# The head of a two-layer diffusion block in single feature blocks: finer adaLN blocks, first projection one feature at a time, sums of squares added on the matrix engine

## The chip, the core and the metric

The kernel runs on one core of one Trainium2 chip. The metric is device time in microseconds (us) of one execution; a profiled execution also gives a span, from the first instruction to the last. Engines: PE (matrix products; PEld loads its weights), DVE (vector), ACT (activation), POOL, and SP, which here only issues DMAs. Each engine runs its own list of instructions in the order in which the program gave them out, and waits at an instruction until its inputs are there.

## The reference, cut to what matters

Two streams of 256 tokens, context and latent, of width 1024, go through two layers. What the change touches is the very beginning of layer 0:

```python
def rms_norm(x, w=None):
    y = x32 * lax.rsqrt(jnp.mean(x32 * x32, axis=-1, keepdims=True) + EPS)
...
    cond = jax.nn.silu(c)
    cond_c = jax.nn.silu(c_ctx)
    h, hc = x, ctx
    for l in range(DEPTH):
        mod = jnp.split((cond @ w_ada[l] + b_ada[l])[:, None, :], 6, axis=-1)
        mod_c = jnp.split(cond_c @ w_ada[l] + b_ada[l], 6, axis=-1)
        a = modulate(rms_norm(h, norm1_w[l]), mod[0], mod[1])
        ac = modulate(rms_norm(hc, norm1_w[l]), mod_c[0], mod_c[1])
        y, y_c = token_mixers(a, ac, ...)
```

So before the first projection can start, three things must exist: the inverse norm of each token, the first two (shift and scale) of the six adaLN vectors, and the modulated input `a`. The projection that comes first in the kernel is the one into the 416 (here 448) columns of latent attention.

## The kernel before, in words

All matrix products of weight kind are done in three passes, since operands are split into a high and a low part: high times high, high times low, low times high. `split` makes the parts of a weight (ACT copies the high part, DVE subtracts), `norm_block` makes those of the modulated input: DVE forms x, ACT adds the shift and writes the high part, DVE writes the low part. The model width of 1024 is eight feature blocks of 128, called f0 to f7 here; the 512 tokens are four tiles, of which tiles 2 and 3 are context (s = 1) and 0 and 1 latent (s = 0).

The head runs so. SP issues the loads, all on one queue: three small ones, then the four pieces of h, the parameters, and then by turns a block of the adaLN weights (four pieces of 512 KB, `load_ada0`) and a unit of the projection's weights (448 KB, `wdma`). At most eight loads are under way: each further one waits for the landing of the load eight places ahead of it. `square_sums` squares h and adds the pieces on DVE, and PE sums over the partitions with a column of ones; `rsqrt1` and `inv_diag` make the inverse norms on DVE; `broadcast` spreads them with PE into the PSUM tile `rb0`. `first_ada(b)` computes adaLN block b on PE, a pair of features in 512 columns, and `first_mod(b)` turns its row into columns (`cp`, small PE products), adds the bias on DVE and calls `norm_block` for both features and streams. `warm` issues products that nobody reads; they keep PE busy while it would wait.

The first projection is `agroup` over four units i = 0 to 3 of two features each. For each unit it goes over the tiles 2, 3, 0, 1 and for each over both features: 24 products of 448 columns, 96 in all. `first_hook` puts the rest of adaLN between them: after the second tile of unit i it calls `first_mod(i + 1)`, after the fourth `first_ada(i + 2)`. `load_rest`, called at the end of `first_ada(2)`, issues the loads of tables that are needed later, among them the mask `msk` (128 KB), which DVE converts at line 159 into the tile `mk`. After the projection come the wide products of the mixers (L229 to L231) and, between them, the preparation of latent attention (`mla_prepare`).

The order on each engine is set when the program is made, by a list scheduler that follows the text of the program and its own clock; `issue_after` pins an instruction behind another.

## Time and profile before

| | before |
|---|---|
| time, median of 3 runs (range) | 1559.16 us (1558.87 to 1565.18) |
| time of the profiled execution | 1562.33 us |
| its span | 1560.6 us |
| PE busy | 1539.3 us, 99% |
| DVE busy | 1182.4 us, 76% |
| ACT busy | 737.8 us, 47% |
| granted PE clock, mean | 0.998 |

A busy share near 100% of one engine says that the other engines matter only where PE waits for them. In the forty slices of the page PE stands at 8 in the first and the last and at 9 in all others, so what can be lost or won around the change lies in the first 60 us. The rows are copied further down.

### The profile page before, as it was taken

What the parts mean: (1) busy time and instruction counts of PE and PEld (TensorE: products, weight loads), DVE (VectorE), ACT (ScalarE), POOL (GpSimd) and SP (SyncE); (2) the same over time, 40 slices, a digit from 0 to 9 for tenths busy, and PEclk for the clock granted to TensorE, in tenths of its full rate; (3) what the DMA queues carried; (4) which work ended last, traced back from release to release, by engine and by line L of the source; (5) the groups of instructions that cost most, each with busy time, mean ns of one, the idle gap of its engine ahead of it and who ended that gap; (6) DMA issues with size and microseconds to landing.
All of it is one profiled execution on the core that took longest, in us unless ns stands there. A gap on an engine that the chain in (4) does not pass through costs nothing.

```text
span 1560.6 us, 25204 instructions
## 1 busy us (share of the span) xinstructions
PE 1539.3 (99%) x9410; PEld 1319.5 (85%) x9411; DVE 1182.4 (76%) x2931; ACT 737.8 (47%) x1504; POOL 13.8 (1%) x53
## 2 busy tenths in 40 slices
PE   8999999999999999999999999999999999999998
PEld 4887677877888889888888889987888799999998
DVE  5894457787899998668876776786688887896764
ACT  3665465353423333532332342556665364675553
POOL 1000000000000000000000000000000000000000
PEclk9999999999999999999999999999999999999999
DMA  9332112221344573236655563432234234555552
GB/s 368 125 108 68 55 46 70 76 77 64 112 154 141 204 259 125 91 121 202 191 190 200 189 194 118 137 106 68 83 99 127 71 133 151 188 164 192 182 185 88
DMA packets 63034, 215.56 MB, mean 138 GB/s; under 512 B 7104, under 2 KB 10560, under 8 KB 62912
## 3 DMA queue, kind: packets, MB, share of 16 engines
q1 hardware_dynamic: 62912, 213.95, 41.4%
q8 instruction: 74, 1.21, 0.3%
q14 instruction: 48, 0.39, 0.1%
HBM read 212.88 MB, written 1.05 MB: 137 GB/s over the span
## 4 chain that ended last, share of the span: by engine, by line
PE 69%; DVE 6%; issue 1%; ACT 1%; DMA 0%; DVEq 0%
PE pm L229 19%; PE pm L231 18%; PE pm L230 18%; PE pm L479 2%; PE pm L481 2%; PE pm L480 2%; PE pd L789 1%; DVE wl L226 1%; PE pd L645 1%; DVE junk L359 1%; PE pd L883 1%; PE pd L892 1%; PE pd L670 1%; DMA ar<-in_wadT_dram 0%; DVE u L742 0%
## 5 line engine op out<-in xcount | busy, mean ns | idle before, releaser
L229 PE MATMUL pm<-u,wh 128*128 128x256 f32 (+1 forms) x1868 | 645.0, 346 | 1.1 <-ACT wh L225 1.1
L231 PE MATMUL pm<-u,wl 128*128 128x256 f32 (+1 forms) x1868 | 632.0, 339 | 1.8 <-DVE wl L226 1.8
L230 PE MATMUL pm<-u,wh 128*128 128x256 f32 (+1 forms) x1868 | 631.8, 339 | 0.0
L225 ACT ACTIVATE wh<-raw 128x512 fp32r<-128x512 f32 (+1 forms) x526 | 310.4, 619 | 447.1 <-PE pm L230 306.1
L226 DVE TENSOR_TENSOR wl<-raw,wh 128x512 fp32r<-128x512 f32 (+1 forms) x526 | 344.8, 679 | 108.0 <-ACT wh L225 103.3
L229 PEld LDWEIGHTS pm<-u,wh 128*128 128x128 f32 x1868 | 354.8, 190 | 41.5 <-issue 3.2
L231 PEld LDWEIGHTS pm<-u,wl 128*128 128x128 f32 x1868 | 354.5, 190 | 40.7 <-DVE wl L226 2.4
L230 PEld LDWEIGHTS pm<-u,wh 128*128 128x128 f32 x1868 | 355.2, 190 | 38.2 <-issue 1.4
L359 DVE SCALAR_TENSOR_TENSOR junk<-ar,crow 128x512 bf16<-128x512 f32 x256 | 166.4, 690 | 4.4 <-DMA ar<-in_wadT_dram 4.4
L479 PE MATMUL pm<-wh,u 128*128 128x512 f32 (+3 forms) x304 | 117.2, 386 | 0.9 <-DVE s L1071 0.9
L481 PE MATMUL pm<-wh,u 128*128 128x512 f32 (+3 forms) x304 | 111.6, 370 | 0.0
L480 PE MATMUL pm<-wl,u 128*128 128x512 f32 (+3 forms) x304 | 111.1, 366 | 0.0
L1181 DVE SCALAR_TENSOR_TENSOR u<-pm,modT,u 128x256 f32<-128x256 f32 x96 | 44.4, 482 | 59.8 <-PE pm L231 59.6
L479 PEld LDWEIGHTS pm<-wh,u 128*128 128x128 f32 x304 | 57.3, 189 | 14.8 <-issue 3.8
L480 PEld LDWEIGHTS pm<-wl,u 128*128 128x128 f32 x304 | 57.4, 189 | 11.4 <-issue 4.7
L481 PEld LDWEIGHTS pm<-wh,u 128*128 128x128 f32 x304 | 57.3, 189 | 9.7 <-issue 1.4
L229 PE MATMUL pm<-u,w 128*128 128x256 f32 (+1 forms) x220 | 62.7, 285 | 0.0
L231 PE MATMUL pm<-u,w 128*128 128x256 f32 (+1 forms) x220 | 62.5, 284 | 0.0
L230 PE MATMUL pm<-u,w 128*128 128x256 f32 (+1 forms) x220 | 62.3, 283 | 0.0
L225 ACT ACTIVATE w<-raw 128x512 fp32r<-128x512 f32 (+1 forms) x68 | 39.1, 611 | 26.7 <-PE pm L230 15.6
L647 DVE TENSOR_REDUCE st<-pd 128x1 f32<-128x512 f32 (+1 forms) x48 | 28.6, 598 | 27.2 <-PE pd L645 26.9
L1270 DVE TENSOR_TENSOR s<-s,pm 128x512 f32<-128x512 f32 (+1 forms) x42 | 23.5, 561 | 33.6 <-PE pm L231 25.1
(263 smaller groups left out, 1906.7 us busy)
## 6 DMA issues: line engine op xcount, KB each, us to landing
raw<-in_wu_dram SPq DMA_DIRECT2D x256, 512.0 KB, 3.5
ar<-in_wadT_dram SPq DMA_DIRECT2D x80, 512.0 KB, 4.2
raw<-in_wu_dram SPq DMA_DIRECT2D x40, 448.0 KB, 3.3
u<-in_wad_dram SPq DMA_DIRECT2D x16, 512.0 KB, 10.1
u<-in_hin_dram SPq DMA_DIRECT2D x8, 512.0 KB, 6.3
raw<-in_wqb_dram SPq DMA_DIRECT2D x4, 384.0 KB, 3.4
raw<-in_wkvb_dram SPq DMA_DIRECT2D x2, 512.0 KB, 5.5
crow<-in_crow_dram SPq DMA_DIRECT2D x2, 512.0 KB, 4.8
```

What stands on the lines that cost most here:

```text
L225: ACT.activation(out=hi, in_=src, func=AF.Copy)
L226: paced[0] = DVE.tensor_tensor(out=lo, in0=src, in1=hi.bitcast(F32), op=ALU.subtract)
L229: PE.matmul(o, lh, rh, start=start, stop=False, **kw)
L230: PE.matmul(o, lh, rl, start=False, stop=False, **kw)
L231: PE.matmul(o, ll, rh, start=False, stop=stop, **kw)
L359: DVE.scalar_tensor_tensor(out=junk[:, sl], in0=raw[:, sl], scalar=1.0, in1=crows[s][:, sl], op0=ALU.mult, op1=ALU.mult, accum_out=part[:, ...
L479: PE.matmul(o, ah, wh, start=first, stop=False)
L480: PE.matmul(o, ah, wl, start=False, stop=False)
L481: PE.matmul(o, al, wh, start=False, stop=last)
L647: DVE.tensor_reduce(out=mx, in_=ps[:, :W], axis=AX.X, op=ALU.max, negate=True)
L1181: DVE.scalar_tensor_tensor(out=hx, in0=ps[:, 256 * s:256 * s + 256], scalar=G[:, f, s:s + 1], in1=hx, op0=ALU.mult, op1=ALU.add)
L1270: DVE.tensor_tensor(out=cv[:, :nq], in0=cv[:, :nq], in1=pu[:, :nq], op=ALU.mult)
```

## The change

The numbers of squares, adaLN weights, products and converted weights stay the same; how they are cut and in which order they stand changes.

- The loads of h go first, the three small loads behind them. The adaLN weights of the first four features are laid out feature by feature; all sixteen pieces and three of the four weight units are issued ahead of the other loads. The parameters of layer 1 move forward, the mask moves behind the weights of latent attention.
- `square_sums`: DVE adds no pieces; PE adds them in PSUM, with 16 one-column products for each stream instead of 4. The inverse norms of the two streams are computed one after the other instead of in one interleaved chain of four.
- adaLN comes in six blocks instead of four: f0, f1, f2, f3 (256 columns each), f4 with f5, f6 with f7 (512 columns each).
- The first two units of the projection go feature by feature over all tiles, the others tile by tile as before. `ADA_AT` and `MOD_AT` say after which (unit, feature of it, tile count) a block and its `first_mod` come.
- The conversion of the projection's weights and `mla_prepare` are pinned behind the norm steps. There are 28 of the products that nobody reads instead of 37.

```diff
     h = {s: load_h(s) for s in (1, 0)}
+    nc.sync.dma_start(out=craw, in_=cond)
+    nc.sync.dma_start(out=cs[:, K_ID:K_ID + 128], in_=cst[:, K_ID:K_ID + 128])
+    nc.sync.dma_start(out=cs[:, K_SEL:K_SEL + 2], in_=cst[:, K_SEL:K_SEL + 2])
...
-        nc.sync.dma_start(out=pr[1], in_=par[1])
...
-            split(hi[:, c0:c1], lo[:, c0:c1], raw[:, c0:c1])
+            held = last_mod if 3 < i < 8 else ()
+            with tc.issue_after(held[0]) if held else nullcontext(), tc.issue_after(held[1]) if held else nullcontext():
+                split(hi[:, c0:c1], lo[:, c0:c1], raw[:, c0:c1])
...
-        wload(i + 1)
+        if i > 2:
+            wload(i + 1)
...
+            if hook and i < 2:
+                for kk in range(2):
+                    for n, t in enumerate(tiles):
+                        product(t, (kk,))
+                        hook(i, kk, n + 1)
+                continue
...
     def square_sums(s):
-        acc = None
...
+        for n in range(4):
+            sq = T3([128, 2, 256])
+            x = h[s][n // 2][:, 2 * (n % 2):2 * (n % 2) + 2]
+            if n % 2 == 0 or (s == 0 and n == 3):
+                ACT.activation(out=sq, in_=x, func=AF.Square)
+            else:
+                paced[0] = DVE.tensor_tensor(out=sq, in0=x, in1=x, op=ALU.mult)
+            for j in range(2):
+                for i in range(2):
+                    with ordered():
+                        ins = PE.matmul(ps[:, j:j + 1], sq[:, i, j * 128:(j + 1) * 128], ones[:, 0:1], start=(n + i + j == 0),
+                                        stop=(n == 3 and i == 1), skip_group_check=True)
+                    seg.append(ins)
...
-    ada0 = [load_ada0(0)]
+    ada0 = [[], [], [], []]
+    load_ada0(0, 0, 2)
     wdma(0)
-    ada0.append(load_ada0(1))
+    load_ada0(0, 2, 4)
+    nc.sync.dma_start(out=pr[1], in_=par[1])
+    load_ada0(1, 0, 2)
     wdma(1)
+    load_ada0(1, 2, 4)
+    load_ada0(2)
+    wdma(2)
+    load_ada0(3)
+
+    BLOCKS = ((0, 1), (1, 1), (2, 1), (3, 1), (4, 2), (6, 2))
...
-        if 0 < b < 3:
-            wdma(b)
-            ada0.append(load_ada0(b + 1))
...
+        if b == 3:
+            wdma(3)
+            load_rest()
...
-        row = ACT.activation(out=first_row[b], in_=ps, func=AF.Copy)
-        if b == 2:
-            wdma(3)
-            load_rest()
+        row = ACT.activation(out=first_row[b][:, :w], in_=ps[:, :w], func=AF.Copy)
...
-    warm(8)
+    warm(6)
     ps0 = square_sums(0)
...
-    row0 = first_ada(0, lambda: warm(4))
...
+    first_ada(0, lambda: warm(2))
+    broadcast(1, dg1)
+    broadcast(0, dg0)
...
-    warm(5)
-    first_ada(1)
...
+    def first_hook(i, kk, n):
+        at = (i, kk, n)
+        if at in ADA_AT:
+            first_ada(ADA_AT.index(at) + 1)
+        if at in MOD_AT:
+            b = MOD_AT.index(at) + 1
+            with tc.issue_after(paced[0].ins):
+                act, dve = first_mod(b)
+            last_mod[:] = act.ins, dve.ins
+            if b in (1, 3, 4):
+                with tc.issue_after(act.ins), tc.issue_after(dve.ins):
+                    wload({1: 1, 3: 2, 4: 3}[b])
+
+    ADA_AT = ((0, 0, 1), (0, 0, 4), (0, 1, 4), (1, 1, 3), (2, 1, 3))
+    MOD_AT = ((0, 0, 2), (0, 1, 2), (1, 0, 2), (1, 1, 4), (2, 1, 4))
...
-        S = mla_prepare(l)
+        with tc.issue_after(last_mod[0]) if full else nullcontext(), tc.issue_after(last_mod[1]) if full else nullcontext():
+            S = mla_prepare(l)
```

How the order on the engines changes is shown at three places. A row is a line of the program, the operation, out<-in by the program's names, and the shape.

The first place is the queue of SP from the last adaLN pieces (`in_wad`) on. Behind them come the fourth weight unit (128x896), tables (`in_cst`), the mask (`in_msk`), the weights of latent attention (`in_wkvb`, `in_wqb`) and the fifth unit (128x1024). Before:

```order
L951 DMA u_414<-in_wad_dram 128x1024
L247 DMA raw_427<-in_wu_dram 128x896
L156 DMA cs<-in_cst_dram 128x128
L158 DMA s_430<-in_msk_dram 128x256
L160 DMA cs<-in_cst_dram 128x1536
L161 DMA pr_96<-in_par_dram 128x262
L247 DMA raw_564<-in_wu_dram 128x1024
L495 DMA raw_596<-in_wkvb_dram 128x1024
L495 DMA raw_604<-in_wqb_dram 128x768
```

And now:

```order
L958 DMA u_158<-in_wad_dram 128x1024
L156 DMA cs<-in_cst_dram 128x128
L247 DMA raw_428<-in_wu_dram 128x896
L160 DMA cs<-in_cst_dram 128x1536
L508 DMA raw_637<-in_wkvb_dram 128x1024
L508 DMA raw_645<-in_wqb_dram 128x768
L247 DMA raw_605<-in_wu_dram 128x1024
L158 DMA s_431<-in_msk_dram 128x256
```

The mask, the 30th load of the program before, is the 35th now, behind the tables, the weights of latent attention and the fifth unit; the same 35 loads stand first in both.

The second place is DVE around the conversion of the mask (`mk`). Before, it stands between the norm steps of f4 and f5 (x is L413, the low part L415, the weight's low part L226):

```order
L413 SCALAR_TENSOR_TENSOR s_478<-u_92,st_468,pd_127 128x256
L415 SCALAR_TENSOR_TENSOR u_125<-s_470,modT_115,u_121 128x256
L415 SCALAR_TENSOR_TENSOR u_125<-s_474,modT_115,u_121 128x256
L413 SCALAR_TENSOR_TENSOR s_482<-u_92,st_468,pd_127 128x256
L159 CAST mk<-s_430 128x256
L415 SCALAR_TENSOR_TENSOR u_125<-s_478,modT_115,u_121 128x256
```

Now it stands between x (L416) and the low part (L418, `u_409`) of f3:

```order
L1012 SCALAR_TENSOR_TENSOR st_464<-modT_115,pr_95 128x2
L416 SCALAR_TENSOR_TENSOR s_467<-u_84,st_464,pd_119 128x256
L416 SCALAR_TENSOR_TENSOR s_471<-u_88,st_464,pd_119 128x256
L159 CAST mk<-s_431 128x256
L418 SCALAR_TENSOR_TENSOR u_409<-s_467,modT_115,u_408 128x256
L418 SCALAR_TENSOR_TENSOR u_409<-s_471,modT_115,u_408 128x256
L225 TENSOR_TENSOR wl_476<-raw_150,wh_475 128x448 x2
```

It moved one pair of features forward, ahead of the low part of f3 and of the third unit's weight.

The third place is PE where the projection goes from one unit to the next. Before, at unit 2 (`wh_443`), the `cp` products of f6 and f7 (L992) have twelve products of the same unit behind them:

```order
L481 MATMUL pm_348<-wh_443,u_125 128x448
L992 MATMUL pd_527<-cs,s_507 128x2 x4
L479 MATMUL pm_349<-wh_443,u_121 128x448
L480 MATMUL pm_349<-wl_444,u_121 128x448
L481 MATMUL pm_349<-wh_443,u_125 128x448
L479 MATMUL pm_349<-wh_443,u_121 128x448
```

Now, from the third feature's partner f3 (`wh_376` with `u_408`, `u_409`) to unit 2 (`wh_475`):

```order
L485 MATMUL pm_342<-wh_376,u_409 128x448
L988 MATMUL pd_496<-u_142,cnd 32x512 x2
L988 MATMUL pd_496<-u_144,cnd 32x512 x2
L988 MATMUL pd_496<-u_146,cnd 32x512 x2
L988 MATMUL pd_496<-u_148,cnd 32x512 x2
L483 MATMUL pm_343<-wh_376,u_408 128x448
L484 MATMUL pm_343<-wl_377,u_408 128x448
L485 MATMUL pm_343<-wh_376,u_409 128x448
L1003 MATMUL pd_510<-cs,s_505 128x2 x4
L483 MATMUL pm_340<-wh_475,u_515 128x448
```

The `cp` products of f4 and f5 (L1003) are the last of unit 1 now, and the next product reads f4 itself (`u_515`); the same holds for f6 and f7 between units 2 and 3. Behind the first 345 of PE's rows, 281 of DVE's, 107 of ACT's and 36 of SP's, the orders of both kernels are the same.

## Rows read from the trace of the kernel before

**Rows 1.** Part 1 of the page: engine, busy us, share, instructions.
```profile
PE 1539.3 (99%) x9410; PEld 1319.5 (85%) x9411; DVE 1182.4 (76%) x2931; ACT 737.8 (47%) x1504; POOL 13.8 (1%) x53
```

**Rows 2.** A stretch: busy of PE, PEld, DVE, ACT, POOL, granted clock, DMA share, GB/s.
```profile
25.00:30.00 5.00, 5.00 (x30) 3.58 (x30) 2.19 (x7) 2.04 (x4) 0.00 (x0) 1.00 1.03 409
```

**Rows 3.** PE's timeline: start, length, line, operation, tiles, count, idle before.
```profile
1.53 6.17 PE L913 MATMUL pd<-resetf,wones 128*128 128x512 bf16 x20 [1.53 <-POOL resetf L179]
9.40 1.02 PE L933 MATMUL pd<-ones,y 128*128 128x1 f32 x8 [1.70 <-DVE y L928]
10.28 1.89 PE L913 MATMUL pd<-resetf,wones 128*128 128x512 bf16 x8
...
21.45 0.47 PE L479 MATMUL pm<-wh,u 128*128 128x448 f32 x1
...
39.13 1.93 PE L972 MATMUL pd<-u,cnd 128*32 128x512 f32 x16
...
43.56 0.95 PE L992 MATMUL pd<-cs,s 128*128 128x2 f32 x8
44.37 0.45 PE L479 MATMUL pm<-wh,u 128*128 128x448 f32 x1
...
51.68 0.37 PE L481 MATMUL pm<-wh,u 128*128 128x448 f32 x1
51.89 0.40 PE L229 MATMUL pm<-u,wh 128*128 128x512 f32 x1
```

**Rows 4.** SP's timeline: the first load, h, and the 35th load.
```profile
0.74 0.40 SPq L138 DMA_DIRECT2D st<-in_cond_dram  x1
...
2.12 1.85 SPq L145 DMA_DIRECT2D u<-in_hin_dram  x4
...
35.53 0.33 SPq L495 DMA_DIRECT2D raw<-in_wqb_dram  x1
```

**Rows 5.** Line 495, issue at 35.5 alone: from issue to landing.
```profile
DMA to landing us min/median/max: 7.5/7.5/7.5
```

**Rows 6.** Line 145, the first piece of h alone: from issue to landing.
```profile
DMA to landing us min/median/max: 3.6/3.6/3.6
```

**Rows 7.** DVE's and ACT's timelines: first norm steps, and the mask's conversion.
```profile
19.46 0.23 DVE L998 TENSOR_TENSOR modT<-pd,pr 128x4 f32<-128x4 f32 x2 [0.26 <-PE pd L992]
...
41.00 0.28 DVE L159 CAST mk<-s 128x256 uint8<-128x256 f32 x1
41.20 0.48 DVE L415 SCALAR_TENSOR_TENSOR u<-s,modT,u 128x256 fp32r<-128x256 f32 x1
...
20.45 1.71 ACT L414 ACTIVATE u<-s,modT 128x256 fp32r<-128x256 f32 x4 [1.97 <-DVE s L413]
```

**Rows 8.** Two stretches of PE alone: busy, granted clock, DMA share, GB/s.
```profile
1213.00:1217.00 4.00, 2.07 (x16) 0.97 0.00 0
1217.00:1220.00 3.00, 3.00 (x17) 0.50 0.00 0
```

**Rows 9.** Products of 256 columns there, from PE's timeline.
```profile
1212.65 0.28 PE L229 MATMUL pm<-u,wh 128*128 128x256 f32 x1
1213.26 0.28 PE L231 MATMUL pm<-u,wl 128*128 128x256 f32 x1
...
1217.62 0.41 PE L231 MATMUL pm<-u,wl 128*128 128x256 f32 x1
1218.68 0.41 PE L230 MATMUL pm<-u,wh 128*128 128x256 f32 x1
```

**Rows 10.** DVE's timeline at a later norm: two inverse norms, first and last steps.
```profile
605.60 0.21 DVE L205 TENSOR_SCALAR st<-pd 128x1 f32<-128x1 f32 x2
...
607.53 0.48 DVE L405 TENSOR_SCALAR s<-cs,st 128x128 f32<-128x128 f32 x2
```

**Rows 11.** Issue to landing: fourth weight unit (issued 26.8), table behind it (64 KB, 28.0).
```profile
DMA to landing us min/median/max: 9.9/9.9/9.9
...
DMA to landing us min/median/max: 8.9/8.9/8.9
```

More of the change, by code (lines that the diff above doesn't have):

```diff
@@ L413, in norm_block @@
         DVE.scalar_tensor_tensor(out=x, in0=hx, scalar=A_, in1=rb, op0=ALU.mult, op1=ALU.mult)
-        ACT.activation(out=hi, in_=x, func=AF.Identity, bias=B_)
-        return DVE.scalar_tensor_tensor(out=lo, in0=x, scalar=B_, in1=hi.bitcast(F32), op0=ALU.add, op1=ALU.subtract)
+        act = ACT.activation(out=hi, in_=x, func=AF.Identity, bias=B_)
+        return act, DVE.scalar_tensor_tensor(out=lo, in0=x, scalar=B_, in1=hi.bitcast(F32), op0=ALU.add, op1=ALU.subtract)
     def norm_half(s, acc, A, B, aT, raw=None):
@@ L480, in agroup @@
                     PE.matmul(o, ah, wl, start=False, stop=False)
-                    PE.matmul(o, al, wh, start=False, stop=last)
-                tick(6 * (c1 - c0) / 2.4)
+                    last_mm[0] = PE.matmul(o, al, wh, start=False, stop=last)
+                tick(3 * len(kks) * (c1 - c0) / 2.4)
+            if hook and i < 2:
[4 more added lines that the diff above has]
+                continue
+            for n, t in enumerate(tiles):
+                product(t, (0, 1))
                 if hook:
-                    hook(i, n + 1)
+                    hook(i, 1, n + 1)
         return pss
@@ L994, in first_mod @@
                 seg.append(ins)
-        f0 = 2 * b
-        md = modT[0][:, 0:2, f0:f0 + 2]
-        for m in range(2):
-            DVE.tensor_tensor(out=md[:, m], in0=cp[:, 2 * m:2 * m + 2], in1=bias_cols(0, m, f0, f0 + 2, 2), op=ALU.add)
-        A = ST(4).rearrange("p (f s) -> p f s", s=2)
+        if f0 % 2 == 0:
+            for x in aT:
+                x.append(U([128, 2, 512], F32R))
+        md = modT[0][:, 0:2, f0:f0 + nf]
+        DVE.tensor_tensor(out=md[:, 1], in0=cp[:, nf:], in1=bias_cols(0, 1, f0, f0 + nf, 2), op=ALU.add)
@@ new lines, in first_mod @@
+        if b == 0:
+            with tc.issue_after(ins.ins):
+                first_split(0)
+        with tc.issue_after(paced[0].ins) if b == 0 else nullcontext():
+            for j in range(nf):
+                for s in (1, 0):
+                    f = f0 + j
+                    hi, lo = aTs(aT, f, 256 * s, 256 * s + 256)
+                    ins = norm_block(h[s][f // 4][:, f % 4], A[:, j, s:s + 1], md[:, 0, j, s:s + 1], rb0[:, 256 * s:256 * s + 256], hi, lo)
+        if b == 0:
+            with tc.issue_after(ins[1].ins):
+                first_split(1)
@@ L1009, with first_split @@
+        return ins
+    def first_split(half):
+        raw, n = raws[0]
+        if not half:
+            loaded[0] = tuple(wp.tile([128, 1024], F32R, tag=x, bufs=3, name=nm(x)) for x in ("wh", "wl"))
+        hi, lo = loaded[0]
+        sl = slice(half * n // 2, (half + 1) * n // 2)
+        split(hi[:, sl], lo[:, sl], raw[:, sl])
+        if half:
+            raws.pop(0)
     warm(20)
     ps1 = square_sums(1)
-    warm(8)
+    warm(6)
     ps0 = square_sums(0)
+    dg1 = inv_diag(ps1)
     with tc.issue_after(paced[0].ins):
-        dg = inv_diag([ps[:, j:j + 1] for ps in (ps1, ps0) for j in range(2)])
```

84 lines of the change are left out of this document (27 added, 57 removed).

## The prediction

> **What bounds the kernel now.** I read the busy shares first: PE works in 99% of the span, the next engine in 76% [rows 1], so only what moves PE moves the time. Then I read PE's own order of time in the first 60 us, because the two programs differ nowhere else. After a start with gaps (the products that nobody reads run until about 7.5 us, and PE then waits for DVE's sums, 1.7 us at 9.40) the first product of the projection comes at 21.45, and from there PE has hardly a gap: the last of the 96 stands at 51.68, the first wide product of the mixers at 51.89 [rows 3]. Between them lie 96 products at 0.21 us each (51.68 to 51.89) = 19.9 us, and some 9 us of adaLN and `cp` work. Third, the loads: in a stretch of that time the DMA engines are full and move 409 GB/s [rows 2]. So the head has two walls, PE's work and a full load queue. In the kernel before, PE's work is the later one. All that follows is the question when the first wide product comes: 51.9 now. Behind it the order on each engine is soon the same, and PE goes on without waits, so I take a shift there to reach the end in full.
>
> **Part 1, h first and sums on PE.** The first piece of h is issued at 0.74 instead of 2.12 [rows 4] and so lands 1.4 us earlier. PE does not profit. The first 20 idle products end where they did, at 7.5 us, and behind them PE now has 16 one-column products per stream instead of 4. Eight records (4 products) took from 9.40 to 10.28, 0.88 us [rows 3], so a stream costs 3.5 us instead of 0.9. 7.5 + 3.5 + six idle products at 0.22 (the first to last of 8 took 1.89 us including the last one's end) 1.3 + 3.5 = 16 us for the second stream's sums. Its inverse norms are a chain of two, 2.4 us by the chain of two elsewhere in the trace, 605.60 to 608.01 [rows 10]. 18.5; broadcast and two `cp` products 0.9; then DVE's bias, half a weight conversion of 0.6 us that now stands in between, x, and ACT's high part: 2.2 us. First product: 21.7, so 0.3 us later than now. It takes 5 us more of PE to save nothing, but nothing was lost either.
>
> **Part 2, finer blocks on PE.** adaLN of 512 columns costs 1.93 us [rows 3]. Half of it in 256 columns costs between 0.97 and 1.93; I take 1.05, as the columns should set it. Before, a half block was done ahead of 21.45; now three half blocks and two whole ones follow the first product: 7.0 us against 6.8. `cp` (0.8 us for four columns, 43.56 to 44.37) is 3.0 against 2.4 us. The products are the same. So PE's work grows by some 0.8 us.
>
> **Part 3, norm steps without cover.** From a `cp` to the first product that reads the feature, DVE and ACT need: 0.2 us from the start of the next thing on PE to DVE's bias (the last record of `cp` ends at 43.56 + 0.95 = 44.51, 0.14 after the product behind it starts, and a step to DVE), then 19.46 to the end of ACT's first high part, 20.45 + 0.5 = 20.95, thus 1.5 us, and a step to PE [rows 7]. Before, twelve products (2.5 us) stood behind each `cp`; for f1 and f2 other products and adaLN still do. For f4 and f6 nothing does: `cp` is the last thing of its unit and the next product reads f4 (or f6) itself. That is 1.75 us of waiting, twice, and about 0.3 us for f3. Without part 4 the first wide product would come at 51.9 + 0.3 + 0.8 + 3.8 = 56.8 minus small change, some 4.6 us later than now. This would be 1564 us.
>
> **Part 4, the mask.** This is the term that decides. DVE's conversion of the mask is a wait of a new size: it stands ahead of the low part of f3, on an engine that runs its list in order, and the mask is now the 35th load instead of the 30th. When does it land? The same 35 loads were the first in the kernel before; the last of them was issued at 35.5 and landed 7.5 us later, at 43.0 [rows 4, 5]. The stream now starts 1.4 us earlier and has three small loads (73 KB, 0.2 us at that rate) in it: 41.8. A lower bound: the sizes by their shapes add up to 15.1 MB; at 409 GB/s [rows 2] this is 36.9 us; the first piece, 512 KB or 1.3 us, landed 3.6 us after its issue [rows 6], so the flow begins at 3.1 and ends at 40.0. I take 41.8, since a stream with all its hiccups was measured.
>
> PE gets to f3 at about 34.5: 21.7, 36 products 7.4 us, three half blocks 3.2, three `cp` 1.3, steps between them 0.9. It can do the products with f3's high part, not those with its low part, and all of PE's list stands behind them; so do, on DVE, the low part itself, the third unit's weight and all later norms. PE waits some 7 us, four times the wait at 9.40. How early PE and DVE came to this place no longer matters: parts 1 and 2 before f3 are swallowed.
>
> From the landing (M = 41.8) to the first wide product: conversion 0.28 and low part 0.48 [rows 7] with their steps, 0.8; nine products of f3, 1.9; adaLN of f4 and f5 2.0; row still on ACT, 0.1; `cp` 0.8; norm steps 1.75; eighteen products 3.9 with small waits for low parts; adaLN of f6 and f7 2.0; six products 1.25; `cp` 0.8; norm steps 1.75; 24 products 5.2. Sum 22.3, so 64.1.
>
> The clock comes on top. [...] A stretch like 1217 to 1220 at 0.50, and a little more, loses 3.3 x (1 - 0.12 / 0.21) = 1.4 us; I add 1.5, between 0 and 4.5 if the two later waits cost a dip each.
>
> Sum: 41.8 + 22.3 + 1.5 = 65.6, against 51.9: 13.7 us later. The profiled execution took 1562.33 us, 1.7 us over its span, and 3.2 us over the median of the runs; by it the time would be 1576, by the median of 1559.16 it is **1573 us**. I see no slack later: PE's remaining waits are short and come from other chains. I forecast slower.
>
> [...] The table issued at 28.0 landed at 36.9, right behind a weight unit issued at 26.8 that landed at 36.7 [rows 11]: 64 KB waited for 448 KB ahead of it, so loads land in the order of their issue here. [...]
>
> **The rivals.**
> - *Mask out of order.* If the mask overtook the queue, it would land as soon as it can be issued (it waits for the load eight places ahead; from that one's landing to its own there are 3.4 MB, 8.3 us, so that is 33.5) plus a landing time like the 3.6 us of a load with an empty queue: 37, with PE waiting 2 us at f3 instead of 7, and no dip. 1573 - 4.8 - 1.5 = 1567. Chance 0.05; the landings in order speak against it.
> - *The conversion holds nothing up* (the mask comes before PE needs f3's low part, that is before 35). Then parts 1 to 3 stand alone: 1564. It needs a stream 7 us faster than the full rate. Chance 0.08.
> - *The head is faster, as it is cut to be.* One feature at a time lets PE start as soon as f0 is ready. If the one-column sums ran as fast as the pieces of h come in, they would end near 10.5 us, with h landed 1.4 us earlier, and the projection would start some 3 us earlier; minus the waits at f4 and f6 that is -1 to 0 us: 1558. It decides at the sums: over 0.17 us per one-column product it is gone, and 0.22 was measured; the mask must be in time too. Chance 0.05. More than 7.8 us can't be won by it: the first product would have to come before 13.7, and the sums alone, at the speed measured, are done at 16.
> - *More dips.* Both waits at f4 and f6 also drop the clock: 1576. Chance 0.12.
>
> **How the numbers follow.** Forecast 1573 with 0.70. Its own bounds are 41.8 or 40.0 for the mask and 0 or 1.5 for the clock: 1570 to 1574. With the dips the upper end is 1577; below, 1565 takes in the overtaking mask and leaves the cases near 1564 and 1558 out. Half a per cent, 7.8 us, is about what a measurement of this kernel can tell from no change. Slower by more than that, over 1567: 0.70 + 0.12 + half of the overtaking mask = 0.84. Within: 0.13. Faster by more: 0.03, for what I have not seen.
>
> **What would show it.** Right: DVE's conversion of the mask starts at 40 to 42 with a long wait that a load ended; PE has one gap of 5 to 8 us between products of f3, then a granted clock near 0.5; gaps of 1.5 to 2 us behind the `cp` of f4 and f6; first wide product at 62 to 67. Wrong: the conversion at about 34 without a wait, or the mask landed before loads issued ahead of it. The sums of squares should end near 16 and the first product come near 21.7; whether they do says who is right on parts 1 and 2, and hardly changes the time.

## The result, and the profile of the changed kernel

| | kernel before | changed kernel |
|---|---|---|
| median of 6 executions each, us | 1561.25 (1558.87 to 1565.18) | 1578.39 (1574.62 to 1581.0) |
| profiled execution, us | 1562.33 | 1575.72 |
| its span, us | 1560.6 | 1573.9 |
| first product of the projection at, us | 21.45 | 27.17 |
| first wide product of the mixers at, us | 51.89 | 65.50 |

The ratio is 1.0109, with a 95% interval of 1.0096 to 1.0121: the changed kernel is 17 us slower. The forecast was 1573 us in a range of 1565 to 1577. The direction and most of the size were right, the time lies 1.4 us above the range. The profiled execution is the second fastest of the six.

The first things to read are again PE's busy time and its granted clock in 40 slices (parts 1 and 2 of the page of the changed kernel).

```profile
PE 1549.0 (98%) x9482; PEld 1331.0 (85%) x9482; DVE 1181.2 (75%) x2933; ACT 735.1 (47%) x1504; POOL 12.5 (1%) x53
...
PEclk7999999999999999999999999999999999999999
```

PE is busy for 9.7 us more than in [rows 1] with 72 instructions more, and the first slice, the head, ran at a granted clock of 0.7. PE's timeline of the head (start, length, line, operation, tiles, count, idle before) shows where:

```profile
1.52 6.04 PE L926 MATMUL pd<-resetf,wones 128*128 128x512 bf16 x20 [1.52 <-POOL resetf L178]
7.39 3.63 PE L940 MATMUL pd<-ones,y 128*128 128x1 f32 x32
10.88 2.11 PE L926 MATMUL pd<-resetf,wones 128*128 128x512 bf16 x6
12.79 6.82 PE L940 MATMUL pd<-ones,y 128*128 128x1 f32 x32
...
27.17 0.74 PE L483 MATMUL pm<-wh,u 128*128 128x448 f32 x1 [1.92 <-ACT u L417]
...
42.05 0.47 PE L483 MATMUL pm<-wh,u 128*128 128x448 f32 x1 [0.16 <-ACT u L417]
...
60.28 0.47 PE L483 MATMUL pm<-wh,u 128*128 128x448 f32 x1 [1.51 <-ACT u L417]
65.50 0.40 PE L228 MATMUL pm<-u,wh 128*128 128x512 f32 x1
```

The same 32 records (16 one-column sums) took 3.63 us for the first stream and 6.82 us for the second. The stretches say why (columns as in [rows 2]); first the changed kernel, then the kernel before:

```profile
4.00:11.00 7.00, 7.00 (x48) 5.16 (x47) 2.08 (x3) 3.24 (x7) 1.36 (x8) 1.00 1.04 401
11.00:17.00 6.00, 6.00 (x28) 5.01 (x25) 2.53 (x23) 0.00 (x0) 0.46 (x2) 0.54 1.03 407
17.00:24.00 7.00, 7.00 (x35) 4.26 (x35) 2.42 (x21) 1.33 (x4) 0.00 (x0) 0.50 1.02 406
24.00:32.00 8.00, 6.08 (x30) 3.93 (x29) 3.25 (x11) 1.37 (x4) 0.00 (x0) 0.50 1.03 408
32.00:41.00 9.00, 9.00 (x70) 6.88 (x71) 5.81 (x20) 3.40 (x8) 2.32 (x8) 1.00 0.88 344
41.00:52.00 11.00, 9.33 (x48) 6.34 (x47) 6.57 (x18) 4.59 (x10) 0.00 (x0) 0.87 0.16 50
```

```profile
11.00:17.00 6.00, 5.03 (x33) 1.91 (x32) 5.07 (x42) 0.07 (x2) 2.26 (x7) 1.00 1.03 416
17.00:24.00 7.00, 6.49 (x36) 3.56 (x36) 5.64 (x18) 3.19 (x7) 0.00 (x0) 1.00 1.03 406
```

From about 11.5 to 32 us PE ran at a granted clock of 0.50, with 1.00 before and behind (the lower and the higher level below). It had not idled: from 4 to 11 it was busy in 7.00 of 7.00 us. In the kernel before, PE was busy less in the same stretches (5.03 of 6.00 and 6.49 of 7.00 us) and kept 1.00.

The timelines of VectorE (DVE) and SyncE (SP) show the mask, on which the forecast stood (on SyncE the issue of the fifth weight unit and of the mask behind it, then the conversion and the low part of f3 on VectorE):

```profile
35.97 0.33 SPq L247 DMA_DIRECT2D raw<-in_wu_dram  x1
36.34 0.43 SPq L158 DMA_DIRECT2D s<-in_msk_dram  x1
```

```profile
41.77 0.29 DVE L159 CAST mk<-s 128x256 uint8<-128x256 f32 x1
42.03 0.89 DVE L418 SCALAR_TENSOR_TENSOR u<-s,modT,u 128x256 fp32r<-128x256 f32 x2
```

The load took 5.3 us from issue to landing, so it landed at 41.67, and the conversion began 0.1 us later, without a wait. That this is so near the forecast's 41.8 is luck. SyncE held the unit ahead of the mask back until 35.97, by the profile 3.9 us of it for VectorE's low parts of an earlier weight unit (L225), which ended at 35.94: the slow head delayed the load itself. In the executions below with an earlier first product (e1, e8, the second one of the changed kernel) the mask was issued at 34.0 and landed at 42.3 to 42.4. In this execution PE came to f3 at 42.05, when the mask had just landed: the slow start had used up all the time for which the mask would have held PE. The first wide product came at 65.50, where 65.6 was forecast, but on another path than the forecast's. From there on nothing changed: the span ends 1573.9 - 65.5 = 1508.4 us later, before 1560.6 - 51.9 = 1508.7.

So one execution agrees with the forecast in its number and not in its cause. The runs had to tell which of the two, the clock or the mask, sets the time, and whether one hides the other. The expectations below use these names. **Theory A** (e1 to e4): the one-column sums take the clock down and this sets the head, while the mask, landing at the same 42 us, only just holds nothing up; either alone taken away gives nothing. Against it stand **the theory of the prediction**, the mask alone, for which early work doesn't matter, and **theory B**, the clock alone. **Theory C** (from the second execution of the changed kernel on): the clock costs up to 10 us in the head, at a time that varies, and the mask is a second wall at 42 us; whichever is later counts. **Rival N:** the clock falls from the number of small products, or from the finer blocks.

### The profile page after: what moved, and what is told of

Its sections match the earlier page's. It is cut to its first block, busy times and chain, and to the rows that moved or that the text cites. A ratio compares the mean times of both kernels' runs of the same rounds, so it can differ in the third digit from the quotient of the medians.

```text
span 1573.9 us, 25350 instructions
## 1 busy us (share of the span) xinstructions
PE 1549.0 (98%) x9482; PEld 1331.0 (85%) x9482; DVE 1181.2 (75%) x2933; ACT 735.1 (47%) x1504; POOL 12.5 (1%) x53
## 3 DMA queue, kind: packets, MB, share of 16 engines
HBM read 212.88 MB, written 1.05 MB: 136 GB/s over the span
## 4 chain that ended last, share of the span: by engine, by line
PE 69%; DVE 5%; issue 1%; ACT 1%; DMA 1%; DVEq 0%
PE pm L228 19%; PE pm L230 19%; PE pm L229 19%; PE pm L483 2%; PE pm L485 2%; PE pm L484 2%; PE pd L802 1%; PE pd L658 1%; DVE junk L362 1%; PE pd L905 1%; PE pd L896 1%; DVE wl L225 1%; PE pd L683 1%; DMA ar<-in_wadT_dram 1%; DVE u L755 0%
## 5 line engine op out<-in xcount | busy, mean ns | idle before, releaser
L225 DVE TENSOR_TENSOR wl<-raw,wh 128x512 fp32r<-128x512 f32 (+1 forms) x526 | 344.0, 676 | 107.1 <-ACT wh L224 102.7
L228 PEld LDWEIGHTS pm<-u,wh 128*128 128x128 f32 x1868 | 354.4, 190 | 41.4 <-issue 3.2
L483 PEld LDWEIGHTS pm<-wh,u 128*128 128x128 f32 x304 | 58.0, 191 | 20.6 <-ACT u L417 6.7
L224 ACT ACTIVATE w<-raw 128x512 fp32r<-128x512 f32 (+1 forms) x68 | 39.0, 610 | 26.8 <-PE pm L229 15.7
```

The source lines that it names most:

```text
L224: ACT.activation(out=hi, in_=src, func=AF.Copy)
L225: paced[0] = DVE.tensor_tensor(out=lo, in0=src, in1=hi.bitcast(F32), op=ALU.subtract)
L228: PE.matmul(o, lh, rh, start=start, stop=False, **kw)
L483: PE.matmul(o, ah, wh, start=first, stop=False)
```

## The experiments

All times are against the kernel before on the same chip (its medians there were 1560.7 to 1562.5 us). "First" and "wide" are the starts of the first product and of the first wide product in the profiled execution.

| run | what is changed | first | wide | median us | ratio, 95% interval |
|---|---|---|---|---|---|
| changed kernel | | 27.17 | 65.50 | 1578.39 | 1.0109 [1.0096, 1.0121] |
| e4_before_pe_sums | before + sums on PE | 29.54 | 59.85 | 1568.15 | 1.0044 [1.0026, 1.0061] |
| e1_dve_adds | VectorE adds | 20.73 | 68.54 | 1577.41 | 1.0105 [1.0074, 1.0136] |
| e2_mask_late | late mask | 23.68 | 61.40 | 1574.75 | 1.0083 [1.0060, 1.0106] |
| e3_adds_and_mask | both | 18.70 | 57.29 | 1567.26 | 1.0038 [1.0027, 1.0050] |
| e5_fill | unread products among the sums | 28.70 | 69.12 | 1577.19 | 1.0101 [1.0087, 1.0114] |
| e8_wide_sums | sums of 128 columns | 21.85 | 65.96 | 1577.47 | 1.0099 [1.0083, 1.0116] |
| e10_wide_and_late | e8 + late mask | 21.89 | 59.56 | 1570.41 | 1.0069 [1.0052, 1.0085] |
| e6_fillers_head | e3 + unread products | 19.43 | 55.74 | 1565.53 | 1.0031 [1.0019, 1.0042] |
| e7_cover | e6 + f4, f6 earlier | 19.43 | 50.45 | 1560.80 | 0.9995 [0.9986, 1.0003] |
| e9_cp_first | e7 + `cp` ahead of a broadcast | 20.07 | 51.13 | 1559.34 | 0.9985 [0.9976, 0.9994] |

### The sums alone, in the kernel before

The kernel before with one part of the change, `square_sums` of the changed kernel, 16 products per stream for 4; with it, two of the eight squares go from ScalarE to VectorE (the loads of h stay where they were):

```diff
-    paced[0] = DVE.tensor_tensor(out=acc, in0=acc, in1=sq, op=ALU.add)
...
-    ins = PE.matmul(ps[:, j:j + 1], acc[:, i, j * 128:(j + 1) * 128], ones[:, 0:1], start=(i == 0), stop=(i == 1))
+    ins = PE.matmul(ps[:, j:j + 1], sq[:, i, j * 128:(j + 1) * 128], ones[:, 0:1], start=(n + i + j == 0),
+                    stop=(n == 3 and i == 1), skip_group_check=True)
```

> The kernel before with one part of the change alone: the pieces of the squares added by PE, 16 one-column products per stream. Theory A: the clock falls in the head here too, behind the first or in the second stream's sums; those take near 7 us instead of 3.5, the first product of the projection comes 6 to 9 us later than 21.45, the time grows by 7 to 10 us. If the products' number is what counts and not the clock: clock high throughout, 5.3 us more of PE of which 2.4 fall into waits, time plus 3 us.

Measured: 0.44% slower, 7 us, as theory A had it. The sums' rows and the first product in PE's timeline, then two stretches:

```profile
7.39 3.63 PE L927 MATMUL pd<-ones,y 128*128 128x1 f32 x32
...
13.65 6.83 PE L927 MATMUL pd<-ones,y 128*128 128x1 f32 x32
...
29.54 0.47 PE L479 MATMUL pm<-wh,u 128*128 128x448 f32 x1
```

```profile
4.00:11.00 7.00, 7.00 (x48) 5.15 (x47) 2.08 (x3) 2.99 (x6) 0.51 (x3) 1.00 1.01 390
11.00:17.00 6.00, 6.00 (x26) 4.48 (x23) 0.30 (x3) 0.16 (x2) 0.88 (x6) 0.54 1.02 412
```

The clock falls at the same place in a kernel that has neither the finer blocks nor the early mask. So the sums are enough to take it down. The first product came 8.1 us later and the first wide one 8.0 us later: in this kernel nothing takes the delay up.

### Each suspect away, and both

e1: the changed kernel with the additions on VectorE again (4 products per stream). e2: the changed kernel with the mask's load and conversion behind the preparation of latent attention (`mla_prepare`), where the kernel doesn't need it yet. e3: both.

```diff
     def load_rest():
         nc.sync.dma_start(out=cs[:, K_C32:K_C32 + 128], in_=cst[:, K_C32:K_C32 + 128])
-        mkf = T2([128, 2, 128])
-        nc.sync.dma_start(out=mkf, in_=msk)
-        DVE.tensor_copy(out=mk, in_=mkf)
...
         S = mla_prepare(l)
+        if full:
+            mkf = T2([128, 2, 128])
+            nc.sync.dma_start(out=mkf, in_=msk)
+            DVE.tensor_copy(out=mk, in_=mkf)
```

> The changed kernel with the sums of squares as before the change: DVE adds the pieces, PE sums with 4 one-column products per stream. Theory A (the 32 one-column products let PE's clock fall to the low level from 11.5 us on, and this sets the head; the mask, which lands at 41.7, only just doesn't hold DVE): the clock stays high in the head, the first product of the projection comes near 17 instead of 27.2, PE reaches f3 near 30 - and now the mask holds it until 41.7. First wide product again at 64 to 66, time within 3 us of the changed kernel. Theory B (the clock alone is the cause, the mask costs nothing anywhere): first wide product near 52, time within 2 us of the kernel before.

> The changed kernel with the load and the conversion of the mask moved behind the preparation of latent attention; all else as changed. Theory A: nothing moves, since in the changed kernel the conversion did not wait: first wide product at 65 to 66, time as the changed kernel within 2 us. The theory of the prediction (the mask is the wait that costs the 14 us): first wide product near 57, time 8 us less.

> Both: DVE adds the pieces, and the mask comes later. Theory A: either alone gives nothing, both together give the whole: first product near 17, no low clock in the head, two waits of 1.5 us at f4 and f6, perhaps a dip of the clock behind one; first wide product near 52, time within 2 us of the kernel before. If the low clock in the head came from something else in the change than the one-column products: low clock from about 11 us again, first wide product over 58.

With VectorE's additions (e1) the head is 6.4 us faster at the first product, and nothing is gained, as theory A expected: VectorE's and PE's timelines now show the forecast's wait.

```profile
42.35 0.29 DVE L159 CAST mk<-s 128x256 uint8<-128x256 f32 x1 [7.27 <-DMA s<-in_msk_dram]
```

```profile
43.09 0.74 PE L485 MATMUL pm<-wh,u 128*128 128x448 f32 x1 [6.93 <-DVE u L418]
```

In time, with 1561 us for 1: both undone leaves 5.9 us (e3). Putting back the sums alone (e2) makes it 13.0, the early mask alone (e1) 16.4, both 17.0. So the sums are worth 7.1 alone and the mask 10.5, but together 11.1 and not 17.6. The 6.5 us between the two are no more than the intervals leave open (some 2 to 5 us on each side, 6.6 for the four together), so the times alone don't settle it. The traces do: e1's first product came 6.4 us earlier and its first wide product 3.0 us later than the changed kernel's. The time up to 42 us is paid once. Neither the mask alone nor the clock alone explains that; "whichever is later" does.

But theory A lacked a part. e1 was to keep the clock up in the head, with the first product near 17; it came at 20.73, and PE was at the lower level from about 14.6 to 24.9 us, behind a wait of 2.06 us that ended at 12.37. e2 met neither expectation: its first wide product, 61.40, lies between the 57 and the 65, and it gained 4.0 us on the changed kernel where one side allowed 2 and the other said 8. e3 missed too, 57.29 for 52 and 5.9 us slower than before instead of 2. What its clock did is taken up further down. e1's loss of 16.4 us also holds stretches at the lower level behind the long wait, 0.65 from 41 to 52 us. Its stretches:

```profile
11.00:17.00 6.00, 4.27 (x29) 1.96 (x29) 5.89 (x45) 1.32 (x4) 2.02 (x7) 0.80 1.03 408
17.00:24.00 7.00, 5.08 (x25) 2.97 (x25) 3.25 (x11) 1.11 (x3) 0.46 (x2) 0.50 1.03 408
...
41.00:52.00 11.00, 7.83 (x33) 3.88 (x33) 3.15 (x10) 0.72 (x2) 0.00 (x0) 0.65 0.13 50
```

### The changed kernel twice more

> The changed kernel a second time, unchanged. The profiled execution took 1575.7 us, the median of its six executions 1578.4. Theory C (the clock in the head is the cost, and when it falls varies between executions): the stretch at the lower level begins at another time or has another length than 11.5 to 32.0 us, the first product lies between 22 and 30 us, and the first wide product between 62 and 70. Rival F (the head is the same in each execution, the spread comes from later): the stretch again begins at 11.5 and lasts 20.5 us, the first product again at 27.2 and the first wide product at 65.5.

> The changed kernel a third time. In the two looks so far the lower level began at 11.5 for 20.5 us (first product 27.2, conversion of the mask without a wait of PE, 1575.7 us) and at 17.2 for 3.4 us and again from 24.0 (first product 23.5, PE waits 4.5 us at f3 for the conversion, 1582.2 us). Theory: a first product before 26 goes with a wait of PE at f3 that ends at 42 to 43 us, a later one without; the first wide product lies between 62 and 72 in both cases. Rival: a first product before 26 and no wait at f3 beyond 1 us, or a wait of over 2 us with a first product behind 27.

The third execution was like the first: first product 27.18, no wait at f3, first wide product 65.68, 1575.13 us. The second took the forecast's path, with VectorE waiting for the mask and PE for VectorE, and 1582.18 us. Its PE and VectorE:

```profile
8.51 3.63 PE L940 MATMUL pd<-ones,y 128*128 128x1 f32 x32
...
13.29 3.63 PE L940 MATMUL pd<-ones,y 128*128 128x1 f32 x32
...
23.45 0.47 PE L483 MATMUL pm<-wh,u 128*128 128x448 f32 x1 [1.93 <-ACT u L417]
...
43.14 0.74 PE L485 MATMUL pm<-wh,u 128*128 128x448 f32 x1 [4.46 <-DVE u L418]
```

```profile
42.40 0.29 DVE L159 CAST mk<-s 128x256 uint8<-128x256 f32 x1 [4.79 <-DMA s<-in_msk_dram]
```

```profile
43.00:52.00 9.00, 7.39 (x33) 3.87 (x33) 2.95 (x10) 1.12 (x3) 0.00 (x0) 0.69 0.19 60
52.00:65.00 13.00, 11.44 (x51) 8.81 (x52) 5.57 (x16) 4.08 (x9) 0.00 (x0) 0.76 0.11 40
65.00:71.00 6.00, 6.00 (x23) 5.39 (x23) 3.74 (x9) 3.53 (x9) 0.00 (x0) 0.72 0.00 1
```

Here the clock stayed up through the sums. It was at the lower level from 17.2 to 20.6 and from 24.0 to 27.6 us, and again around the waits at f3, f4 and f6: 0.69, 0.76 and 0.72 from 43 to 71 us. That is the dearer place. A low clock ahead of the mask's landing is hidden behind the mask; behind it, each us counts, and the first wide product came at 70.85. The first and the third execution had one such dip behind 42 us, some 3.4 us long, at the wait ahead of f4 (0.87 from 41 to 52 us in the first).

### What in the sums takes the clock down

e5 puts one unread product of 512 columns behind each four sums; e8 leaves number, order and weights of the 64 sums and gives each 128 columns of ones instead of one.

```diff
 e5:
                     seg.append(ins)
+            warm(1)
...
 e8:
-    ins = PE.matmul(ps[:, j:j + 1], sq[:, i, j * 128:(j + 1) * 128], ones[:, 0:1], start=(n + i + j == 0),
+    ins = PE.matmul(ps[:, 128 * j:128 * j + 128], sq[:, i, j * 128:(j + 1) * 128], ones, start=(n + i + j == 0),
...
```

> The changed kernel with one unread product of 512 columns behind each four of the one-column sums, eight more products of about 0.21 us in all; the 64 sums stay. Theory C (the clock falls because PE has only one-column products to do for several us): no stretch at the lower level begins before 20 us, the second stream's sums take 3.6 us and not 6.8 beside their fillers, the first product moves from 27.2 to 22 to 24.5 us. PE then reaches f3 near 38 and waits some 4 us for the conversion behind the mask, which lands near 41.7, so that the first wide product stays at 63 to 66 and the time at 1573 to 1577. Rival N (the number of small products, or the finer blocks, take the clock down, whatever stands between them): a stretch at the lower level begins near 11.5 again and the first product comes at 28 or later, the time at 1578 or more.

> The changed kernel with the same 64 sums, each against all 128 columns of ones instead of one: number, order and weights of PE's products stay, only their columns change (256-column fp32 products stand at a pitch of 0.12 us in the head, one-column ones at 0.11, so 32 of them take 3.6 to 4.2 us). Run e5 showed that a wide product behind each four sums does not keep the clock. Theory W (it is the single column: PE loads weights and multiplies next to nothing): the clock stays at the higher level through the sums, the first stretch at the lower level begins behind 20 us, the first product comes at 21.5 to 23.5. PE then waits for the conversion of the mask, so the time stays at 1573 to 1577. Theory K (any product this short does it, PE's time goes to loading weights): the lower level begins between 11 and 17 us as before and lasts 10 us or more, first product at 23.5 to 29, time 1577 to 1581.

e5 missed theory C and came near rival N: the clock fell near 12 us all the same, the first product came at 28.70, and the second stream's sums took 1.70 us for 8 records against 0.95 for the first stream's. Single wide products among the sums were not enough here.

e8 hit theory W, but for 0.5 us of its time (1577.47 us). Its PE, VectorE, the stretch of its second sums and that of its wait at f3:

```profile
7.78 3.73 PE L940 MATMUL pd<-ones,y 128*128 128x128 f32 x32
...
12.64 3.73 PE L940 MATMUL pd<-ones,y 128*128 128x128 f32 x32
...
21.85 0.47 PE L483 MATMUL pm<-wh,u 128*128 128x448 f32 x1 [1.92 <-ACT u L417]
...
43.17 0.74 PE L485 MATMUL pm<-wh,u 128*128 128x448 f32 x1 [6.09 <-DVE u L418]
...
65.96 0.39 PE L228 MATMUL pm<-u,wh 128*128 128x512 f32 x1
```

```profile
42.43 0.29 DVE L159 CAST mk<-s 128x256 uint8<-128x256 f32 x1 [6.43 <-DMA s<-in_msk_dram]
```

```profile
11.00:17.00 6.00, 6.00 (x52) 4.83 (x51) 3.04 (x29) 1.04 (x2) 0.83 (x6) 1.00 1.03 413
...
41.00:52.00 11.00, 7.32 (x36) 4.38 (x37) 4.27 (x13) 1.84 (x4) 0.00 (x0) 0.75 0.14 51
```

As many products, as long (3.73 us against 3.63), nearly as much loading of weights (PEld 4.83 of 6 us, against 5.01 and 5.37 in the first and the second execution of the changed kernel) and the clock at 1.00. Number and order of the sums, the weights and the finer blocks are the same, so rival N falls: it was the single column. When the clock falls varies, so one execution would not do. But both traced executions with these sums (e8 and e10, below) kept it until 22.6 us, behind the wait ahead of the first product, and all six with 64 one-column sums lost it before, at 11.5 to 12.1 us or at 17.2 to 17.6. The kernel is not faster by the wider sums, because the mask now takes 6.1 us of PE: 0.99% slower, about as much as the changed kernel's 1.09%.

e10 is e8 with the mask late as well, the changed kernel without clock loss in the sums and without the mask, which is the forecast's intermediate sum of 56.8 us:

> The sums against 128 columns of ones and, beside it, the late mask: the changed kernel without its clock loss in the sums and without its wait at f3, but with the same number of sums on PE and the two uncovered norms. Theory C with the prediction's own parts 1 to 3 (56.8 us for the first wide product without the mask, 4.9 later than the kernel before): first product at 21.5 to 22.5, no stretch at the lower level before 20 us, first wide product at 56.5 to 58.5 (dips behind the three waits of 2 us cost 0 to 2 us), time 4.6 to 6.6 us above the kernel before on that chip, a ratio of 1.003 to 1.004. Rival (the sums on PE cost by their number also at the higher level): first wide product at 60 or later, a ratio of 1.0055 or more.

The first wide product came at 59.56, between the two expectations, the ratio 1.0069 in the rival's range. But the number of sums isn't it: the first product came at 21.89. The stretches show what it was:

```profile
4.00:17.00 13.00, 12.95 (x93) 9.68 (x93) 5.46 (x33) 4.29 (x9) 1.83 (x10) 1.00 1.02 400
...
22.00:32.00 10.00, 10.00 (x68) 6.64 (x72) 5.77 (x17) 3.14 (x8) 0.00 (x0) 0.83 1.02 408
...
43.00:52.00 9.00, 8.46 (x42) 6.17 (x42) 3.93 (x9) 3.32 (x7) 0.00 (x0) 0.81 0.17 58
```

Behind the wait before the first product (1.93 us) and behind the one at f4 (1.50 us, ending at 43.53) the clock dropped for some 3.4 us each (0.17 of 10 us and 0.19 of 9 us are missing, at 0.50). That is 1.7 us each, 3.4 of 59.56: without them 56.2, against the forecast's 56.8. This execution is the fastest of e10's four, 1.5 us under the median; the others have no trace.

### What is left: idle PE and two norms without cover

e6 takes e3 and puts unread products where PE idles (8 for 6 and 4 for 2 in the sums and the first adaLN block, 4 between the broadcasts, 8 ahead of the first product). e7 adds cover for the norms of f4 and f6: `ADA_AT` and `MOD_AT`, the places where a block's adaLN and coefficients come, half a feature earlier.

```diff
 e6:
+    warm(4)
     broadcast(0, dg0)
     with tc.issue_after(paced[0].ins):
         first_mod(0)
+    warm(8)
 e7:
-    ADA_AT = ((0, 0, 1), (0, 0, 4), (0, 1, 4), (1, 1, 3), (2, 1, 3))
-    MOD_AT = ((0, 0, 2), (0, 1, 2), (1, 0, 2), (1, 1, 4), (2, 1, 4))
+    ADA_AT = ((0, 0, 1), (0, 0, 4), (0, 1, 4), (1, 0, 4), (2, 1, 1))
+    MOD_AT = ((0, 0, 2), (0, 1, 2), (1, 0, 2), (1, 1, 2), (2, 1, 2))
```

> The run with DVE's additions and the late mask, with more unread products in the head: 8 for 6 between the streams, 4 for 2 in the first adaLN block, 4 between the broadcasts, 8 behind the first coefficients; they lie where PE is idle there (1.2 and 1.9 us) or cost 0.2 us each. Theory C (what is left of the loss there is the lower level from 17.2 to 27.4 us, and the two norms of f4 and f6 behind their coefficients): no stretch at the lower level in the head, first product at 18 to 19.5, first wide product at 52 to 54 for 57.3, time 1561 to 1563.5, no slower than before by more than 0.3%. Rival N (256-column adaLN blocks take the clock down by themselves): the stretch at the lower level comes again within 17 to 30 us, the first wide product stays at 56 to 58, the time at 1566 to 1568.

> The last one with the coefficients of f4 and f6 taken half a feature earlier, so that products stand between them and the first use of their norms. Theory C: the two waits of 1.76 us of PE at f4 and f6 are gone, the first wide product comes 3 to 3.5 us ahead of that of the last run, at 49 to 50.5, and the time is 1558 to 1560, 1 to 3 us below the kernel before. Rival R (the rows or weights of those blocks arrive only then, so that the wait moves to the adaLN products or the split): the first wide product stays within 1 us of that of the last run, with a new wait of PE ahead of the products of f4 or f6.

Around its first products e3 ran at 0.65 and 0.63, e6 at 1.00 in the same stretches. These are e3's, then e6's:

```profile
16.00:20.00 4.00, 2.08 (x9) 1.46 (x8) 3.15 (x11) 1.00 (x3) 0.46 (x2) 0.65 1.02 407
20.00:30.00 10.00, 10.00 (x58) 6.80 (x58) 3.57 (x13) 2.61 (x6) 0.00 (x0) 0.63 1.03 406
```

```profile
16.00:20.00 4.00, 3.82 (x20) 1.93 (x18) 2.83 (x13) 1.56 (x4) 0.46 (x2) 1.00 1.03 409
20.00:30.00 10.00, 10.00 (x84) 7.05 (x84) 6.20 (x18) 3.79 (x9) 0.00 (x0) 1.00 1.02 406
36.00:46.00 10.00, 8.49 (x45) 6.48 (x45) 4.83 (x13) 3.35 (x7) 1.22 (x7) 0.83 0.66 256
```

So here the clock fell with idle PE time too (busy 2.08 of 4.00 us from 16 to 20 in e3, 3.82 in e6), with only four sums per stream on PE, and the 256-column blocks by themselves (rival N here) did not take it down. e6 was still 2 us slower than expected; its last row shows the reason, a dip of the same kind behind the wait at f4 (1.51 us, ending at 39.54). In e7 both waits are gone and so is the dip: the first wide product comes 5.3 us earlier (50.45 for 55.74), where the two waits alone are 3.0 us. The time falls by 0.36%, to that of the kernel before (0.9995, with 1 in its interval), 0.8 us above the expected 1558 to 1560.

e9 takes e7 and puts the first coefficients ahead of the second broadcast, which `first_mod` now calls behind its `cp` products:

```diff
     broadcast(1, dg1)
-    warm(4)
-    broadcast(0, dg0)
+    warm(2)
     with tc.issue_after(paced[0].ins):
-        first_mod(0)
-    warm(8)
+        first_mod(0, lambda: broadcast(0, dg0))
+    warm(5)
```

> The best version so far (DVE's additions, late mask, unread products, coefficients of f4 and f6 earlier) with the first coefficients ahead of the second broadcast, which today stand behind it though their row is there 1.5 us sooner; two unread products between the broadcasts for four, five behind them for eight. Theory C: VectorE finds the coefficients done when the second broadcast ends, the first product comes at 18.2 to 18.7 for 19.4, the first wide product at 49 to 49.7 for 50.45, the time 1559.5 to 1560.5, 1 to 2 us below the kernel before. Rival R (the first product waits for the split of its weights or the norm's first step anyway, or the clock falls since there are fewer unread products): first product at 19.2 or later, or a stretch at the lower level before 40 us, time 1561 or more.

The ratio is 0.9985, 2.3 us under the kernel before, with an interval that leaves out 1; the median is 1559.34 us. It is the one kernel here whose whole interval lies under the kernel before. But the profiled execution doesn't show the reason I gave, and has the signs of rival R, though not its time: its first product came at 20.07, not at 18.5, with 0.72 of the clock from 11 to 17 us after an idle time of 1.26 us; its first wide product, 51.13, is not earlier than e7's. That e9 is faster than e7 is not shown; that the rebuilt head is no slower than the kernel before is, and for e9 this one interval says a little faster.

## Why the prediction was right and wrong, step by step

In short, two prices of the clock failed: the one-column sums at the full clock (Part 1), which changed the path up to 42 us but hardly the time, and the "+1.5" for the clock behind the waits, which took 6.2 us in the one slower execution that has a trace and put it beyond the range.

- **What bounds the kernel**: right. The shift at the first wide product (13.6 us) is the shift of the span (13.3 us), and the later part takes as long as before (1508.7 us) within 4 us in every traced execution, 1504.7 to 1511.7 us.
- **Part 1** failed, in the clock it was priced at. Its "7.5 + 3.5 + 1.3 + 3.5 = 16 us" takes the second stream's sums at the rate of [rows 3], 0.11 us a record, at the full clock. Measured was 3.63 us, then 6.82 us at a clock of 0.50, the inverse norms later by it, blocks and `cp` slower too, and the first product at 27.17 for 21.7. Where the clock stayed up, with 128 columns, the sum was right to 0.2 us: 21.85 in e8 and 21.89 in e10. For the time it made little difference, since the first wide product came at 65.50 for 65.6: the loss lay ahead of 42 us, where PE would have waited. The view that could have warned is [rows 8]: I read it as "idle time costs clock" and priced a run of one-column products as full work because the profile calls PE busy there.
- **Part 2** was right within what can be seen; 16 records of 256 columns took 1.07 us at the full clock (e6, e7), where I took 1.05.
- **Part 3** was right in its waits: 1.50 or 1.51 us of idle at f4 and at f6 in each run that kept them, against 1.75 counted from where the next record would have started. It lacked the clock: behind such a wait it falls in some executions (at f4 in all three of the changed kernel and in e1, e2, e5, e6 and e10, at f6 in the second one and e5) and not in others (neither in e3 nor e8). A dip cost some 1.4 to 1.7 us, those at f4 in the second execution and e5 3.1.
- **Part 4, the mask**: the landing was right to 0.6 us where the queue ran as forecast, 42.3 to 42.4 for 41.8 (e1, e8 and the second execution); the 41.67 of the first came by a mask issued 2.3 us later on a queue that VectorE had held up. That PE waits there was right in one of three executions of the changed kernel (4.46 us) and in e1 (6.93) and e8 (6.09), whose first products came at 20.73 to 23.45 us; the "early work doesn't matter" was right as well, since e1's first product, 6.4 us earlier, gained nothing. It was wrong that this is always the later wall: with the low clock, PE reaches f3 at the same 42 us by itself.
- **The clock behind the wait**, "+1.5, between 0 and 4.5": e8, with 42.41 for the landing and 65.96 for the wide product, took 23.55 us for the forecast's 22.3 + 1.5 = 23.8, with one dip behind the wait at f3 (43.2 to 46.4 us, so 1.6 us lost). The first execution's 65.50 - 41.67 = 23.8 is the same number by another way: no wait at f3, and a dip at f4 instead. The second execution took 70.85 - 42.38 = 28.5, 6.2 more than 22.3, with dips behind all three waits (2.4, 3.1 and 1.7 us lost). So this term was mis-sized: 1.5 in the sum and 4.5 at most, where 6.2 was measured. It was my estimate from [rows 8, 9], and no run shows it as a fixed price: behind the wait at f3 1.6 us were lost in e8 and 2.4 in the second execution. The rival "more dips" (1576, chance 0.12) named it, with too small a price and chance.
- **The base**: the forecast put 13.7 us on the median of three runs, 1559.16, and gave 1576 by the profiled execution, which came out at 1575.72. The median of all runs beside it was 1561.25, so 2.1 us of the 5.4 that are missing lie there, and 3.3 us in executions slower than the profiled one, like the second. Only three executions of the changed kernel have a trace; that the others above 1577 us are of its kind is likely, not shown.
- **The order of landings**: in this case the mask landed behind the unit issued just ahead of it (5.4 us from its issue at 35.97, thus 41.4, the mask at 41.67; in e8 the unit at 42.1, the mask at 42.4), so neither shows the mask overtaking; the rival *Mask out of order* did not come.
- **"A faster head"** (1558, chance 0.05, if a sum cost less than 0.17 us): the condition was named rightly, but its own sum doesn't give 1558: 3 us earlier, with two waits of 1.75 us and Part 2's 0.8 us against it, is 1.3 us later than before, not 0 to 1 earlier. The first piece of h did land earlier in the changed kernel (4.3 us, before 2.12 + 3.6 = 5.7 by [rows 4, 6]), but what makes the head no slower is the opposite of the change: additions on VectorE, the mask late, unread products, and cover at f4 and f6 (e7, e9).

What stays open: why the clock falls near 11.5 us in four traced executions with 64 one-column sums (two of the changed kernel, e4 and e5), and only near 17 us in two others (the second one and e2). In those two the 20 unread products at the start took 7.15 and 7.35 us, in the four 6.03 to 6.31 (6.41 and 6.45 in e8 and e10), so the time of the fall goes with something that lies ahead of the sums. Open is also why a wait of 1.5 us costs a dip in one execution and not in the next.

## What to carry to other kernels

Price PE work by the clock it will run at: here a PE busy in 7.00 of 7.00 us went from 1.00 to 0.50 behind 3.63 us of one-column products, and a dip behind a wait of 1.5 us cost 1.4 to 3.1 us more. When two walls stand one behind the other (here 42 us by the loads and 42 us by PE), take each away alone and then both, since each hides the other's gain. Before an input's load is put ahead of critical ones, find what its first use stands in front of in the list of its engine (here VectorE's wait of 4.79 to 7.27 us for the mask stood in front of f3's low part, and PE then waited 4.46 to 6.93 us).

## What the runs showed of the hardware

- A PE that the profile calls busy without a gap went from a granted clock of 1.00 to 0.50 at 11.5 us, behind 3.63 us of one-column fp32 products (changed kernel: busy 7.00 of 7.00 us from 4 to 11, then a clock of 0.54 from 11 to 17 and 0.50 from 17 to 24); the same products with 128 columns, 3.73 us and with the same weight loads, kept 1.00 (from 4 to 17 us in e8 and e10). So a PE that the profile calls busy did not keep the clock by that alone.
- A sum against 128 columns cost hardly more than one against a single column: 3.73 against 3.63 us for 32 records, 0.003 us each.
- Stretches at the lower level (0.50) lasted from 3.4 to 20.5 us in the head, and began at different times in executions of the same program (11.5, 17.2 and 11.9 us in three of the changed kernel).
- A load was late because of the engine that freed the buffer of the load ahead of it: SyncE issued the mask at 36.34 us behind a unit that, by the profile, waited 3.9 us for VectorE, and at 34.0 us in three executions where it did not.
